# RWKV-7 chunk steps: the state kept in U's half of the tile, brought into the bank of its update by identity products

## The chip, the cores and the metric

One core of a Trainium2 chip runs the whole kernel. The metric is the device time of one execution in microseconds; the median of three runs is given. The engines are TensorE (matmuls and transposes, results in PSUM), VectorE, ScalarE, GpSimd and the DMA queues. PSUM has 8 banks of 128 partitions by 512 fp32 values here, shared by all stages through one pool.

## The reference

A trunk of two layers over 512 tokens of width 1024: an RG-LRU block, a conv-MLP, an RWKV-7 time-mixing block, a second conv-MLP, a final norm. The change lies in the RWKV-7 scan, 16 heads of 64:

```python
def step(S, inp):
    r_t, w_t, k_t, v_t, a_t, b_t = inp
    sa = jnp.einsum('bhij,bhj->bhi', S, a_t)
    S = S * w_t[:, :, None, :] + sa[..., None] * b_t[:, :, None, :] + v_t[..., :, None] * k_t[..., None, :]
    y = jnp.einsum('bhij,bhj->bhi', S, r_t)
    return S, y
```

## The kernel before

**The scan in chunks.** The 512 tokens are cut into 8 chunks of 64. Within a chunk the recurrence is written with matrices: a triangular system per head and chunk, solved beforehand (`solve`, whose inverse stands in `LTs`), gives U, the rows that the old state contributes through `a`; then y and the new state are products with U, v and the old state. The heads are handled in halves H (8 heads each) and each half in two groups g of 4 heads. Group 1 runs one step behind group 0, so there are 17 steps n = 0 to 16, and step n handles chunk n of group 0 and chunk n - 1 of group 1 (8 chunks of H = 0, then 8 of H = 1). Chunks of even and odd number use opposite halves of the 128 partitions (`q`), so that a state written in one step is read in place in the next.

**One step.** `step(n)` issues, in this order:
- `pe` (L1206): 8 products, 128 rows by 64 columns, of the masked matrix `W` with the tile `sv`, which has v in one half of its partitions and the state S in the other. ScalarE copies the result to `e1` (L1209).
- `prep_begin` and `prep_s` for step n + 1: 64-row products `s` (L1160) into two banks, which VectorE multiplies with masks into the next `W` (L1167).
- `fill(0)`: work of other stages that is spread over the steps. Three lanes of generators hold it: the v projection of the second half and the first half of the output projection (`acc`), the solve of H = 1, which has long rows of small VectorE operations (L1041, L1043), the bonus terms (`bon`) and the gate (`pgt`). `fills` says how many pieces of each lane go into each of a step's three places.
- `pu` (L1222) and the first products of `py` (L1225), 64 rows by 64 columns, alternating; `py` reads the state from `sv`. ScalarE copies `pu` into `tu` as U (L1229).
- `prep_t` for step n + 1: four transposes `tr` (L1174), ScalarE's copies of them to `tok` (L1176), of `rts` (L1180), of v beside U (L1183), and VectorE's copy of v into the next `sv` (L1184).
- `fill(1)`.
- `pd` (L1238): the update of the state by U and v, 8 products. VectorE adds the old state (L1247) and multiplies with the decay (L1248) into the next `sv`; after a first chunk, where the state is zero, it multiplies straight out of PSUM (L1250).
- The last products of `py` (L1254), and ScalarE's copies of `py` to `ytok` (L1258).
- `between()`, which advances the tail of earlier chunks (group norm, `mu`, `var`, `ytok`, `pz`), and `fill(2)`.

**The order.** The Tile framework turns this program into one static list for each engine. Operations keep roughly the program's order; one that is ready earlier can be placed ahead of others, except where `keep_in_program_order` ties it. Every engine runs its list in order, and semaphores follow from what tiles are read and written. PSUM tiles of the pool share 8 banks, so a new tile waits for a bank to come free.

The tiles that matter: `svs`, two state-and-v tiles; `W` and `tu` for each step, from a pool of 21 buffers, `tu` holding `tok` and `uv` (v in one half of the partitions, U in the other).

Of the kernel before, what the change touches and what calls it, by code (L numbers as in the profile page):

```python
# [7 lines left out]
F32 = mybir.dt.float32  # L8
F32R = mybir.dt.float32r
AF = mybir.ActivationFunctionType  # L10
ALU = mybir.AluOpType
# [4 lines left out]
P = 128  # L16
# [5 lines left out]
C = 64  # L22
NC = T // C
# [18 lines left out]
class Kernel:  # L42
# [1042 lines left out]
    def rwkv_chunks(self, pool, mv, AR, BK, PC, selk, LTs, again):  # L1085
# [9 lines left out]
        nc, tc, I = self.nc, self.tc, self.I  # L1095
        V = self.x.rearrange("p k t -> p (k t)").rearrange("p (c n) -> p c n", c=4)
        half = lambda i: slice(i * 64, i * 64 + 64)

        svs = [pool.tile([P, 4, 2, C], F32, name=f"sv{i}") for i in range(2)]
        rts = pool.tile([P, 4, C], F32, name="rts")  # L1100
        e1 = pool.tile([P, 2, 2, C], F32, name="e1")
        decay = pool.tile([P, KB, 2, NC], F32, name="decay")
# [15 lines left out]
        sets, ytok = {}, {}  # L1118
# [11 lines left out]
        def groups(n):  # L1130

            out = []
            for g in range(2):
                m = n - g
                if 0 <= m < 2 * NC:
                    H, c = m // NC, m % NC
                    out.append((g, slice(2 * g, 2 * g + 2), H, c, c // 2, c % 2))
            return out

        def prep_begin(n):  # L1140
            W, tu = self.b4(F32, (2, 4, P), "W"), self.b4(F32, (2, 4, P), "tu")
            sets[n] = (W, tu[:, 0], tu[:, 1])
            for g, bs, H, c, c2, q in groups(n):
                if c == 0:
                    nc.gpsimd.memset(svs[n % 2][half(1 - q), bs], 0.0)

        def prep_s(n):
            gs = groups(n)
            W = sets[n][0]
            pss = [four(self.bank("s")) for _ in range(2)]  # L1150

            for i in range(2):
                for part in range(3):
                    for g, bs, H, c, c2, q in gs:
                        for h in range(2):
                            b, z = 2 * g + i, 1 - q if part else q
                            row = slice(q * P + z * C, q * P + z * C + C)
                            col = (slice(0, P), half(q), half(1 - q))[part]
                            w = self.ident[half(h), half(h)] if part == 2 else BK[H][half(h), b, c2, row]
                            nc.tensor.matmul(pss[h][half(z), b, col], w, AR[H][half(h), b, c2, q * P + col.start : q * P + col.stop],  # L1160
                                             start=True, stop=True, tile_position=(h * 64, z * 64))

            q0, g0, k = gs[0][5], gs[0][0], len(gs)
            mask = masks[:, q0 : q0 + k].rearrange("p q z t -> p q (z t)").unsqueeze(2).to_broadcast([P, k, 2, P])
            two = lambda t: t[:, 2 * g0 : 2 * (g0 + k)].rearrange("p (g i) t -> p g i t", i=2)
            for h in range(2):
                nc.vector.tensor_tensor(two(W[:, h]), two(pss[h]), mask, ALU.mult)  # L1167
        def prep_t(n):
            gs = groups(n)
            W, tok, uv = sets[n]  # L1170
            pt = four(self.bank("tr"))
            for g, bs, H, c, c2, q in gs:
                for i in range(2 * g, 2 * g + 2):
                    nc.tensor.transpose(pt[:, i, :], BK[H][:, i, c2, q * P : (q + 1) * P], self.ident)  # L1174
            bs = slice(gs[0][1].start, gs[-1][1].stop)
            nc.scalar.copy(tok[:, bs], pt[:, bs])  # L1176
            for g, bs, H, c, c2, q in gs:
                bh = half(1 - q)

                nc.scalar.copy(rts[bh, bs], AR[H][half(q), bs, c2, q * P + q * C : q * P + (q + 1) * C])  # L1180
                n0 = H * 512 + g * 256
                v = V[half(q), c2, n0 : n0 + 256].rearrange("p (i t) -> p i t", t=P)
                nc.scalar.copy(uv[half(q), bs], v)  # L1183
                nc.vector.tensor_copy(svs[n % 2][half(q), bs].rearrange("p i h t -> p i (h t)"), v)  # L1184

        def fill(i):
            for lane in range(3):
                self.background(self.fills[lane][i], lane)

        def step(n, between):  # L1190
            gs = groups(n)
            W, tok, uv = sets.pop(n)
            sv = svs[n % 2]
            more = n < 2 * NC

            heads = [(i, h, G) for i in range(2) for h in range(2) for G in gs]

            late = [(i, h, G) for i in range(2) for h in range(2) for G in gs[::-1]]
            chained = lambda first, ins: ins if first else tc.keep_in_program_order(ins)
            by_head = lambda ps: ps[:, 0:256].rearrange("p (i h t) -> p i h t", h=2, t=C)  # L1200
            flat = lambda t: t.rearrange("p i h t -> p i (h t)")

            pe = by_head(self.bank("pe"))
            for n_, (i, h, (g, bs, H, c, c2, q)) in enumerate(late):
                bh = half(1 - q)
                chained(n_ == 0, nc.tensor.matmul(pe[bh, i, h], W[:, h, 2 * g + i, bh], sv[:, 2 * g + i, h], start=True, stop=True,  # L1206
                                                  tile_position=(0, 64 - q * 64)))
            of = slice(0, P) if len(gs) == 2 else half(1 - gs[0][5])
            nc.scalar.copy(e1[of], pe[of])  # L1209

            if more:
                prep_begin(n + 1)
                prep_s(n + 1)
            if n == NC + 1:

                between()
            fill(0)

            pu, py = by_head(self.bank("pu")), by_head(self.bank("py"))
            for i, h, (g, bs, H, c, c2, q) in heads:  # L1220
                kh, bh, b = half(q), half(1 - q), 2 * g + i
                nc.tensor.matmul(pu[bh, i, h], LTs[H][bh, c2 * 8 + b * 2 + h, :], e1[bh, i, h], start=True, stop=True,  # L1222
                                 tile_position=(64 - q * 64, 64 - q * 64))
                r = rts[bh, b] if h == q else AR[H][bh, b, c2, q * P + q * C : q * P + q * C + C]
                tc.keep_in_program_order(nc.tensor.matmul(py[kh, i, h], r, sv[bh, b, h], start=i + h == 0, stop=False,  # L1225
                                                          tile_position=(64 - q * 64, q * 64)))
            for g, bs, H, c, c2, q in gs:
                bh = half(1 - q)
                nc.scalar.copy(uv[bh, bs], flat(pu[bh]))  # L1229
            if more:  # L1230
                prep_t(n + 1)
            fill(1)
            if any(c < NC - 1 for g, bs, H, c, c2, q in gs):
                pd = by_head(self.bank("pd"))
                live = [x for x in late if x[2][3] < NC - 1]
                for n_, (i, h, (g, bs, H, c, c2, q)) in enumerate(live):
                    b = 2 * g + i
                    chained(n_ == 0, nc.tensor.matmul(pd[half(1 - q), i, h], tok[:, b, half(h)], uv[:, b, half(h)], start=True, stop=True,  # L1238
                                                      tile_position=(0, 64 - q * 64)))
                for g, bs, H, c, c2, q in gs:  # L1240
                    if c == NC - 1:
                        continue
                    kh, bh = half(q), half(1 - q)
                    Sn = svs[1 - n % 2][kh, bs]
                    w = decay[:, H * 4 + 2 * g : H * 4 + 2 * g + 2, :, c : c + 1].to_broadcast([P, 2, 2, C])
                    if c:
                        nc.vector.tensor_tensor(Sn, pd[bh], sv[bh, bs], ALU.add)  # L1247
                        nc.vector.tensor_tensor(Sn, Sn, w[kh], ALU.mult)  # L1248
                    else:
                        nc.vector.tensor_tensor(Sn, pd[bh], w[bh], ALU.mult)  # L1250
            for n_, (i, h, (g, bs, H, c, c2, q)) in enumerate(late):
                kh, b = half(q), 2 * g + i
                chained(n_ == 0 and not any(c < NC - 1 for _, _, _, c, _, _ in gs),
                        nc.tensor.matmul(py[kh, i, h], W[:, h, b, kh], uv[:, b, half(h)], start=False, stop=i + h == 2, tile_position=(0, q * 64)))  # L1254
            for g, bs, H, c, c2, q in gs:
                if g == 0 and q == 0:
                    ytok[H, c2] = pool.tile([P, 4, P], F32, tag="ytok", name="ytok", bufs=3)
                nc.scalar.copy(ytok[H, c2][half(q), bs], flat(py[half(q)]))  # L1258
            between()
            fill(2)  # L1260
# [265 lines left out]
```

## Time and profile before

| what | value |
|---|---|
| median of 3 runs | 1327.06 us (1325.48 to 1329.35) |
| profiled execution, its own time | 1328.46 us |
| its span | 1326.7 us |
| TensorE (PE) busy | 1295.2 us, 98% |
| VectorE (DVE) busy | 860.3 us, 65% |
| ScalarE (ACT) busy | 614.0 us, 46% |
| mean granted clock of TensorE | 0.992 |

Busy times of TensorE come from records of which two belong to one fp32 matmul; records overlap, so starts tell more than durations. Times inside the trace count from the span's start. A figure in brackets behind a row is the idle time of that engine before it, with the instruction that ended it.

### The profile page before, as it was taken

Reading aid. Unit: us, or ns where it says so; the run is one execution under the profiler, and the core shown is the slowest. Engines: PE = TensorE matmul, PEld = TensorE weight load, DVE = VectorE, ACT = ScalarE, POOL = GpSimd, SP = SyncE. Lnnn points to the kernel's source line nnn. Section 1 sums busy time; section 2 is a strip of 40 time slices with the busy share of each in tenths; the row PEclk is TensorE's granted clock in tenths of the full one; section 3 lists DMA queues with packets and bytes.
Section 4 is the critical chain, followed back from the end, with each engine's and each line's share of the span. In section 5 each row is a group of like instructions: output and inputs, shape, how many; then the busy total and the mean of one; then the engine's idle time right before and its main releaser. Section 6 shows DMA issues by size and latency. Waiting matters only on the chain.

```text
span 1326.7 us, 20245 instructions
## 1 busy us (share of the span) xinstructions
PE 1295.2 (98%) x8339; PEld 1055.3 (80%) x8339; DVE 860.3 (65%) x1332; ACT 614.0 (46%) x968; POOL 67.9 (5%) x110
## 2 busy tenths in 40 slices
PE   8999999999999999999999988799999999999998
PEld 7877888888888888876678877678888888888886
DVE  5998656455436655497989787877565555365523
ACT  6797444333224423368843668555533332244311
POOL 4000000000000000020010011120000000000000
PEclk8999999999999999999999999899999999999999
DMA  5423333323333433213212112133323223333311
GB/s 183 126 64 96 96 111 96 95 64 96 95 96 95 127 115 120 88 32 116 86 48 72 58 38 80 42 89 91 99 89 109 67 95 95 96 96 127 112 64 64
DMA packets 72124, 120.27 MB, mean 91 GB/s; under 512 B 9498, under 2 KB 21476, under 8 KB 71904
## 3 DMA queue, kind: packets, MB, share of 16 engines
q1 hardware_dynamic: 70672, 117.20, 28.7%
q8 instruction: 65, 1.06, 0.3%
q10 hardware_dynamic: 576, 1.05, 0.2%
q0 software_dynamic: 784, 0.74, 0.2%
q14 instruction: 27, 0.22, 0.1%
HBM read 114.44 MB, written 4.52 MB: 90 GB/s over the span
## 4 chain that ended last, share of the span: by engine, by line
PE 88%; DVE 6%; ACT 3%; issue 1%; DMA 1%; POOL 0%; SPq 0%; POOLq 0%; DVEq 0%; ACTq 0%
PE acc L51 22%; PE acc L53 22%; PE acc L52 22%; PE acc L616 3%; PE acc L615 3%; PE acc L617 3%; PE s L1160 1%; PE acc L989 1%; PE acc L990 1%; PE acc L991 1%; PE pe L1206 1%; DVE W L1167 1%; DMA xin<-in_x_dram 1%; DVE X L1043 1%; DVE sv L1248 1%
## 5 line engine op out<-in xcount | busy, mean ns | idle before, releaser
L51 PE MATMUL acc<-xs,wh 128*128 128x512 f32 x896 | 352.0, 393 | 0.0
L53 PE MATMUL acc<-xs,wl 128*128 128x512 f32 x896 | 348.9, 390 | 0.7 <-DVE wl L91 0.7
L52 PE MATMUL acc<-xs,wh 128*128 128x512 f32 x896 | 349.6, 390 | 0.0
L91 DVE TENSOR_TENSOR wl<-raw,wh 128x1024 fp32r<-128x1024 f32 (+1 forms) x201 | 242.9, 1216 | 163.4 <-PE acc L52 95.0
L90 ACT CAST wh<-raw 128x1024 fp32r<-128x1024 f32 (+1 forms) x201 | 207.9, 1045 | 257.7 <-DVE wl L91 169.6
L53 PEld LDWEIGHTS acc<-xs,wl 128*128 128x128 f32 x896 | 168.5, 188 | 36.8 <-DVE wl L91 1.2
L51 PEld LDWEIGHTS acc<-xs,wh 128*128 128x128 f32 x896 | 168.8, 188 | 35.0 <-ACT wh L90 0.2
L52 PEld LDWEIGHTS acc<-xs,wh 128*128 128x128 f32 x896 | 168.7, 188 | 34.5 <-DVE wl L91 0.2
L576 DVE SCALAR_TENSOR_TENSOR cv<-gpad,pv,cv 128x512 f32<-128x512 f32 x96 | 71.9, 749 | 22.2 <-ACT cv L574 21.1
L90 ACT CAST hid<-un 128x512 fp32r<-128x512 f32 x48 | 29.8, 620 | 108.7 <-DVE un L583 108.7
L616 PE MATMUL acc<-wh,hid 128*128 128x512 f32 (+1 forms) x200 | 76.8, 384 | 0.0
L615 PE MATMUL acc<-wh,hid 128*128 128x512 f32 (+1 forms) x200 | 76.5, 382 | 0.0
L617 PE MATMUL acc<-wl,hid 128*128 128x512 f32 (+1 forms) x200 | 75.9, 380 | 0.0
L52 PE MATMUL acc<-hid,wh 128*128 128x512 f32 x192 | 75.7, 394 | 0.0
L53 PE MATMUL acc<-hid,wl 128*128 128x512 f32 x192 | 75.6, 394 | 0.0
L51 PE MATMUL acc<-hid,wh 128*128 128x512 f32 x192 | 75.5, 393 | 0.0
L582 DVE TENSOR_TENSOR un<-acc,rb 128x512 f32<-128x512 f32 x48 | 33.1, 689 | 44.3 <-PE acc L53 44.3
L91 DVE TENSOR_TENSOR hid<-un,hid 128x512 fp32r<-128x512 f32 x48 | 33.2, 691 | 31.5 <-ACT hid L90 31.5
L574 ACT ACTIVATE cv<-gpad,pv 128x512 f32<-128x512 f32 x48 | 39.2, 817 | 20.3 <-DVE gpad L571 20.1
L578 ACT ACTIVATE ge<-cv 128x512 f32<-128x512 f32 x48 | 30.1, 627 | 35.6 <-DVE cv L576 35.6
L620 DVE TENSOR_TENSOR xtok<-xtok,acc 128x512 f32<-128x512 f32 (+1 forms) x25 | 16.7, 666 | 44.9 <-PE acc L617 44.9
L615 PEld LDWEIGHTS acc<-wh,hid 128*128 128x128 f32 x200 | 37.5, 188 | 8.0
(425 smaller groups left out, 2176.1 us busy)
## 6 DMA issues: line engine op xcount, KB each, us to landing
raw<-in_ffn_w_up_dram SPq DMA_DIRECT2D x96, 512.0 KB, 3.9
raw<-in_ffn_w_down_dram SPq DMA_DIRECT2D x48, 512.0 KB, 3.7
raw<-in_rwkv_w_rkv_dram SPq DMA_DIRECT2D x24, 512.0 KB, 3.8
raw<-in_lru_w_in_dram SPq DMA_DIRECT2D x16, 512.0 KB, 3.9
raw<-in_lru_w_out_dram SPq DMA_DIRECT2D x8, 512.0 KB, 3.8
raw<-in_rwkv_w_out_dram SPq DMA_DIRECT2D x8, 512.0 KB, 3.4
xd<-x SPq DMA_DIRECT2D x8, 256.0 KB, 2.0
AR<-xd SPq DMA_DIRECT2D x1, 2048.0 KB, 9.1
```

Of the source, the lines that this page charges most:

```text
L51: nc.tensor.matmul(ps, wh, xh, start=start, stop=False)
L52: nc.tensor.matmul(ps, wh, xl, start=False, stop=False)
L53: nc.tensor.matmul(ps, wl, xh, start=False, stop=stop)
L90: (self.nc.vector.tensor_copy if dve else self.nc.scalar.copy)(hi, src)
L91: self.nc.vector.tensor_tensor(lo, src, hi.bitcast(F32), ALU.subtract)
L574: nc.scalar.activation(cv, gp[:, 0:T], AF.Identity, bias=self.vec(f"ffn_conv_b{l}", fb), scale=cw(0))
L576: nc.vector.scalar_tensor_tensor(cv, gp[:, j : j + T], cw(j), cv, ALU.mult, ALU.add)
L578: nc.scalar.activation(ges[o], cv, AF.Gelu_apprx_tanh)
L582: nc.vector.tensor_tensor(un, ps, rbs[0], ALU.mult)
L615: nc.tensor.matmul(ps, hh[:, s], wh[:, k, m], start=kk == 0, stop=False)
L616: nc.tensor.matmul(ps, hl[:, s], wh[:, k, m], start=False, stop=False)
L617: nc.tensor.matmul(ps, hh[:, s], wl[:, k, m], start=False, stop=kk == 7)
```

## The change

The separate tiles `svs` go. The state S now stands in `uv`, in the half of the partitions where U of the same step will be written; `pe` and the first products of `py` read it there, beside v, which ScalarE already copies into `uv`. VectorE's copy of v goes. Before `pu`, 64-row products with the identity put S into the bank `pd` (for groups that have a state and another chunk to come); the later products of U and v accumulate onto it, so the addition L1247 goes, and one VectorE product with the decay writes the new state from PSUM into the next step's `uv`. The memset that clears the state at a first chunk writes to the next `tu`.

```diff
-        svs = [pool.tile([P, 4, 2, C], F32, name=f"sv{i}") for i in range(2)]
...
         def prep_begin(n):
-            W, tu = self.b4(F32, (2, 4, P), "W"), self.b4(F32, (2, 4, P), "tu")
-            sets[n] = (W, tu[:, 0], tu[:, 1])
+            W, tu = self.b4(F32, (2, 4, P), "W"), self.b4(F32, (2, 4 * P), "tu")
+            sets[n] = (W, *(tu[:, i].rearrange("p (i t) -> p i t", t=P) for i in range(2)))
             for g, bs, H, c, c2, q in groups(n):
                 if c == 0:
-                    nc.gpsimd.memset(svs[n % 2][half(1 - q), bs], 0.0)
+                    nc.gpsimd.memset(tu[half(1 - q), 1, bs.start * P : bs.stop * P], 0.0)
...
                 nc.scalar.copy(uv[half(q), bs], v)
-                nc.vector.tensor_copy(svs[n % 2][half(q), bs].rearrange("p i h t -> p i (h t)"), v)
...
-                chained(n_ == 0, nc.tensor.matmul(pe[bh, i, h], W[:, h, 2 * g + i, bh], sv[:, 2 * g + i, h], start=True, stop=True,
+                chained(n_ == 0, nc.tensor.matmul(pe[bh, i, h], W[:, h, 2 * g + i, bh], uv[:, 2 * g + i, half(h)], start=True, stop=True,
...
             fill(0)
+
+            live = [x for x in late if x[2][3] < NC - 1]
+            if live:
+                pd = by_head(self.bank("pd"))
+            for i, h, (g, bs, H, c, c2, q) in live:
+                kh, bh = half(q), half(1 - q)
+                if c:
+                    nc.tensor.matmul(pd[kh, i, h], self.ident[bh, bh], uv[bh, 2 * g + i, half(h)], start=i + h == 0, stop=False,
+                                     tile_position=(64 - q * 64, q * 64))
...
-                tc.keep_in_program_order(nc.tensor.matmul(py[kh, i, h], r, sv[bh, b, h], start=i + h == 0, stop=False,
+                tc.keep_in_program_order(nc.tensor.matmul(py[kh, i, h], r, uv[bh, b, half(h)], start=i + h == 0, stop=False,
...
             fill(1)
-            if any(c < NC - 1 for g, bs, H, c, c2, q in gs):
-                pd = by_head(self.bank("pd"))
-                live = [x for x in late if x[2][3] < NC - 1]
-                for n_, (i, h, (g, bs, H, c, c2, q)) in enumerate(live):
-                    b = 2 * g + i
-                    chained(n_ == 0, nc.tensor.matmul(pd[half(1 - q), i, h], tok[:, b, half(h)], uv[:, b, half(h)], start=True, stop=True,
-                                                      tile_position=(0, 64 - q * 64)))
-                for g, bs, H, c, c2, q in gs:
-                    if c == NC - 1:
-                        continue
-                    kh, bh = half(q), half(1 - q)
-                    Sn = svs[1 - n % 2][kh, bs]
+            for n_, (i, h, (g, bs, H, c, c2, q)) in enumerate(live):
+                b = 2 * g + i
+                chained(n_ == 0, nc.tensor.matmul(pd[half(q), i, h], tok[:, b, half(h)], uv[:, b, half(h)], start=c + i + h == 0, stop=i + h == 2,
+                                                  tile_position=(0, q * 64)))
+            for g, bs, H, c, c2, q in gs:
+                if c < NC - 1:
+                    kh = half(q)
                     w = decay[:, H * 4 + 2 * g : H * 4 + 2 * g + 2, :, c : c + 1].to_broadcast([P, 2, 2, C])
-                    if c:
-                        nc.vector.tensor_tensor(Sn, pd[bh], sv[bh, bs], ALU.add)
-                        nc.vector.tensor_tensor(Sn, Sn, w[kh], ALU.mult)
-                    else:
-                        nc.vector.tensor_tensor(Sn, pd[bh], w[bh], ALU.mult)
+                    Sn = sets[n + 1][2][kh, bs].rearrange("p i (h t) -> p i h t", h=2)
+                    nc.vector.tensor_tensor(Sn, pd[kh], w[kh], ALU.mult)
```

## Rows read from the trace of the kernel before

**Rows 1.** The page's slices: busy tenths in 40 equal parts of the span.

```profile
PE   8999999999999999999999988799999999999998
DVE  5998656455436655497989787877565555365523
```

**Rows 2.** Windows from `pe` to `pe`, steps 1 and 14: busy us of each engine.

```profile
core 0: us, PE busy (x) PEld busy (x) DVE busy (x) ACT busy (x) POOL busy (x), PEclk, DMA share, GB/s
...
747.07:757.34 10.27, 8.60 (x160) 6.19 (x159) 9.67 (x24) 5.25 (x12) 0.00 (x0) 1.00 0.21 73
...
866.97:874.57 7.60, 7.60 (x148) 5.94 (x149) 6.86 (x13) 5.16 (x13) 0.00 (x0) 1.00 0.46 140
```

**Rows 3.** Waits, 738 to 887 us: us in total, times, longest.

```profile
ACT rts L1180 <- PE py L1225: 13.3, 11, 2.9
...
PE pe L1206 <- DVE sv L1248: 6.7, 7, 2.9
```

**Rows 4.** Timeline of TensorE: start, us, line, out<-in, count, idle time before.

```profile
757.34 0.87 PE L1206 MATMUL pe<-sv,W 128*64 128x64 f32 x12 [1.67 <-DVE sv L1250]
...
779.06 1.08 PE L1206 MATMUL pe<-sv,W 128*64 128x64 f32 x16 [2.95 <-DVE sv L1248]
...
799.39 0.69 PE L1206 MATMUL pe<-sv,W 128*64 128x64 f32 x16 [0.69 <-DVE sv L1248]
...
803.70 1.20 PE L1065 MATMUL m1p<-XN,O 32*32 32x32 f32 x64 [1.51 <-DVE XN L1048]
...
831.68 1.12 PE L1288 MATMUL pz<-ident,ytok 128*128 128x128 f32 x4 [2.94 <-DVE ytok L1283]
...
851.25 0.69 PE L1206 MATMUL pe<-sv,W 128*64 128x64 f32 x16 [1.88 <-DVE sv L1248]
```

**Rows 5.** Groups of instructions, 738 to 887 us: count, busy us, mean ns, idle before.

```profile
L1248 DVE TENSOR_TENSOR sv<-sv,decay 64x256 f32<-64x256 f32 x24 | 10.6, 440 | 0.6
...
L1247 DVE TENSOR_TENSOR sv<-pd,sv 64x256 f32<-64x256 f32 x24 | 10.1, 422 | 9.3 <-PE pd L1238 8.8
...
L1184 DVE COPY sv<-x 64x256 f32<-64x256 f32 x28 | 9.3, 331 | 3.3 <-PE pe L1206 2.8
...
L1250 DVE TENSOR_TENSOR sv<-pd,decay 64x256 f32<-64x256 f32 x4 | 1.7, 426 | 0.6 <-PE pd L1238 0.5
```

**Rows 6.** Timeline of VectorE, end of step 1.

```profile
756.32 0.42 DVE L1247 TENSOR_TENSOR sv<-pd,sv 64x256 f32<-64x256 f32 x1
756.77 0.43 DVE L1250 TENSOR_TENSOR sv<-pd,decay 64x256 f32<-64x256 f32 x1
```

**Rows 7.** Timeline of TensorE, steps 0 and 2.

```profile
740.06 0.68 PE L1206 MATMUL pe<-sv,W 128*64 128x64 f32 x8
...
740.67 0.56 PE L1160 MATMUL s<-AR,BK 64*64 64x128 f32 x16
...
762.21 0.27 PE L1222 MATMUL pu<-e,LT 64*64 64x64 f32 x1
...
762.83 0.66 PE L1174 MATMUL tr<-ident,BK 128*128 128x128 f32 x4
...
764.13 0.69 PE L1238 MATMUL pd<-tu 128*64 128x64 f32 x16
...
764.64 0.64 PE L1254 MATMUL py<-tu,W 128*64 128x64 f32 x16
```

**Rows 8.** Timeline of ScalarE, step 4.

```profile
782.73 0.30 ACT L1180 COPY rts<-AR 64x128 f32<-64x128 f32 x1 [1.12 <-PE py L1225]
783.04 0.74 ACT L1229 COPY tu<-pu 64x256 f32<-64x256 f32 x2
...
787.44 0.82 ACT L1183 COPY tu<-x 64x256 f32<-64x256 f32 x2
```

**Rows 9.** Windows after two of the gaps; the third figure from the end is the granted clock.

```profile
757.30:762.20 4.90, 4.80 (x74) 4.34 (x74) 4.71 (x10) 1.36 (x4) 0.85 (x1) 0.65 0.35 110
...
779.00:784.00 5.00, 4.74 (x106) 4.38 (x108) 2.31 (x5) 2.63 (x6) 1.99 (x2) 0.66 0.01 3
```

**Rows 10.** Timelines of TensorE and VectorE in step 4: the transposes, the mask products.

```profile
782.74 0.66 PE L1174 MATMUL tr<-ident,BK 128*128 128x128 f32 x4
...
786.62 1.28 DVE L1167 TENSOR_TENSOR W<-s,masks 128x512 f32<-128x512 f32 x2
```

More of the change, by code (lines that the diff above doesn't have):

```diff
@@ L1192, in step @@
             W, tok, uv = sets.pop(n)
-            sv = svs[n % 2]
             more = n < 2 * NC
@@ L1232, in step @@
             fill(1)
-            if any(c < NC - 1 for g, bs, H, c, c2, q in gs):
-                pd = by_head(self.bank("pd"))
-                live = [x for x in late if x[2][3] < NC - 1]
-                for n_, (i, h, (g, bs, H, c, c2, q)) in enumerate(live):
-                    b = 2 * g + i
-                    chained(n_ == 0, nc.tensor.matmul(pd[half(1 - q), i, h], tok[:, b, half(h)], uv[:, b, half(h)], start=True, stop=True,
-                                                      tile_position=(0, 64 - q * 64)))
-                for g, bs, H, c, c2, q in gs:
-                    if c == NC - 1:
-                        continue
-                    kh, bh = half(q), half(1 - q)
-                    Sn = svs[1 - n % 2][kh, bs]
-                    w = decay[:, H * 4 + 2 * g : H * 4 + 2 * g + 2, :, c : c + 1].to_broadcast([P, 2, 2, C])
-                    if c:
-                        nc.vector.tensor_tensor(Sn, pd[bh], sv[bh, bs], ALU.add)
-                        nc.vector.tensor_tensor(Sn, Sn, w[kh], ALU.mult)
-                    else:
-                        nc.vector.tensor_tensor(Sn, pd[bh], w[bh], ALU.mult)
+            for n_, (i, h, (g, bs, H, c, c2, q)) in enumerate(live):
[5 more added lines that the diff above has]
+                    kh = half(q)
+                    w = decay[:, H * 4 + 2 * g : H * 4 + 2 * g + 2, :, c : c + 1].to_broadcast([P, 2, 2, C])
+                    Sn = sets[n + 1][2][kh, bs].rearrange("p i (h t) -> p i h t", h=2)
+                    nc.vector.tensor_tensor(Sn, pd[kh], w[kh], ALU.mult)
             for n_, (i, h, (g, bs, H, c, c2, q)) in enumerate(late):
                 kh, b = half(q), 2 * g + i
-                chained(n_ == 0 and not any(c < NC - 1 for _, _, _, c, _, _ in gs),
+                chained(n_ == 0 and not live,
                         nc.tensor.matmul(py[kh, i, h], W[:, h, b, kh], uv[:, b, half(h)], start=False, stop=i + h == 2, tile_position=(0, q * 64)))
```

## The prediction

> **What bounds the kernel now.** I read the page's slices first [rows 1]: TensorE is at nine tenths nearly everywhere, but falls to 8, 8 and 7 in the slices from 763 to 862 us, where VectorE stands at 7 and 8. That is where the RWKV steps are: 17 steps, from the first `pe` products at 740.06 us to the last at 881.20 us. No engine is full throughout, so the stage has to be read step by step.
>
> Windows cut at the `pe` products give that; two of the sixteen are shown [rows 2]. In step 1 VectorE is busy for 9.67 of 10.27 us and TensorE for 8.60; up to step 3 and in steps 5, 6, 11 and 12 VectorE is busy for 94 to 98%. In step 14 TensorE is full, and after the steps it stays so to the end: what the stage saves, the end saves.
>
> The list of waits names what TensorE waits for [rows 3]: the state product L1248, seven times, 6.7 us. The timeline places it [rows 4]: `pe` begins after idle gaps of 1.67 us (step 2, behind L1250, the same product for a first chunk), 2.95 (step 4), 0.69 (step 6) and 1.88 (step 12). Four smaller gaps make up the rest of the 6.7, 1.2 us. Two more gaps end in VectorE: 1.51 us before the solve's `m1p` in step 6 and 2.94 before `pz` in step 9.
>
> **What is removed.** In the stage, 24 additions (L1247) of 422 ns and 28 copies of v (L1184) of 331 ns mean [rows 5]: 10.1 + 9.3 = 19.4 us of VectorE. With its spacing an addition takes 0.45 us (starts at 756.32 and 756.77 [rows 6]), and a copy, most of which take 0.28 us, about 0.30. A step with two additions loses 1.5 us of VectorE, step 1, with one, 1.05. All of them stand ahead of the next state product in VectorE's queue. Where VectorE is full the step can shorten by all of this; where it is not, only the additions count, which lie between `pd` and `pe`.
>
> **What is added.** Identity products, 4 for each group that has a state: 24 times, 96 products, in 14 steps (1 to 7 and 9 to 15). The nearest rows are `pd` and the `py` behind it, 8 products each in two parts of the array, two records a product: `pd` begins at 764.13, `py` at 764.64 [rows 7], so 0.51 us for 16 records. One group alone is no cheaper: its `pe`, 8 records, takes from 740.06 to 740.67, 0.61 us. From below, `pu` and the early `py`, 32 records in four parts, take 0.62 us (762.21 to 762.83), which is 0.31 for 16. I take 0.51, since the identity products use only the two parts that early `py` uses. For 14 steps: 4.3 us from below, 7.1 taken, 8.5 from above, and nothing where TensorE idles anyway.
>
> The state product now reads `pd` in PSUM. The kernel has four of that kind already, L1250: 426 ns mean, against 440 for L1248 [rows 5]. I take no difference. [...]
>
> **What is moved or newly waited for.** The state stands in U's half, so the U copy (L1229) must also wait for `pe`, the early `py` and the identity products. On ScalarE the copy to `rts` waits for that `py` already, 11 times [rows 3], and in step 4, at 782.73, it stands right ahead of U [rows 8]. So the new wait ends with a product that ScalarE waits for anyway. Behind U in ScalarE's queue are the `tok` copy and the next `rts`; they come no later for it than `pu` itself does. I take zero. The copy of v beside U (L1183) now precedes `pe` of the next step: the tightest case is two copies that start at 787.44 and last 0.82 [rows 8], ending 0.57 us before `pe` at 788.83. With that cover gone `pe` would wait for ScalarE. The memset that clears the state goes to a fresh tile on GpSimd; no instruction waits for it before. No DMA is issued or moved. The bank of `pd` is held from before `pu`: nothing here, weighed below.
>
> **The sum, by step.** A step's new length is the longer of TensorE's time plus 0.51 and VectorE's less 1.5.
> - Where TensorE waited for VectorE: step 1, min(1.05, 1.67 - 0.51) = 1.05. Step 3, min(1.50, 2.95 - 0.51) = 1.50. Steps 5 and 6 together, 0.69 + 1.51 less two identity groups = 1.2 (VectorE's 3.0 suffices). Step 11, min(1.5, 1.88 - 0.51) = 1.37. Together 5.1 us.
> - Where TensorE had little idle time, steps 2, 4, 7, 10 and 12 to 15: 8 x 0.51, less the small gaps of 1.2 us and one of 0.15 before step 5 that the profile gives to the sequencer: 2.7 us lost.
> - Step 9: `pd` waits there for a ScalarE that is busy, which covers the identity products, and two copies go from ahead of the reductions whose result `pz` waits for: 0.5 us gained.
> - The clock. [...] By the terms above the first gap shrinks to 0.11 us, the second to 0.94. I count the first loss as gone and the second as halved: 2.5 us gained. Bounds 0 and 3.4.
>
> 5.1 - 2.7 + 0.5 + 2.5 = 5.4 us. The profiled execution took 1328.46 us (its span is 1326.7), so 1323.1; it lies 1.4 us above the runs' median of 1327.06, hence 1321.7, rounded to **1322 us**.
>
> **The rivals.**
> *TensorE takes it back.* The identity products cost 0.61 each time, 1.4 us more in 14 steps, and the clock falls as before: 5.1 - 2.7 + 0.5 - 1.4 = 1.5 us gained, 1325.6. For it: `pe`, which other shapes follow, takes 0.61 where `pd`, which its own shape follows, takes 0.51 [rows 7]. Against it: as written the identity products have the shape of `pu` behind them. [...]
>
> *VectorE held up more.* All the idle time that ended in the state products and in `m1p` closes (6.7 + 1.67 + 1.51 = 9.9), half of that before `pz` (1.5) and both clock losses (3.4), less 7.1 for the identity products: 7.7 us, and more if other orders on VectorE follow: 1317 to 1319. Against it: in steps 3 and 11 the removed work is smaller than the gap.
>
> *A ninth PSUM bank: slower.* With `pd`'s bank held from before `pu`, those held when `tr` asks for its own are two of `s`, two of `acc`, `pu`, `py` and `pd`: seven, and `tr` takes the eighth and last. If one more is held there (`bon`, as in step 1), TensorE stops at `tr` until VectorE's mask product frees a bank of `s`. That comes late: in step 4 `tr` starts at 782.74, the two mask products at 786.62 for 1.28 us [rows 10]. To the middle of the two, less the additions of 0.9 us, this is 3.6 us; three more steps of that kind (1, 5 and 6) make some 3.4. The gains of steps 3, 5 and 6 go, and half of the clock's stays (1.3): 1.05 + 1.37 + 0.5 + 1.3 - 2.7 - 7.0 = 5.5 us lost, 1332.5. It decides as soon as a ninth bank is wanted in steps 4 to 6. Against it: the count gives eight, and `tr` never has a gap before it now. [...]
>
> **How the numbers follow.** Forecast 0.43 (own range 1319 to 1325), TensorE takes it back 0.25, VectorE held up more 0.17, the ninth bank 0.15. A measurement of this kernel tells about 0.3%, 4.0 us, from no change: faster is below 1323.1, slower above 1331.0. Faster: two thirds of the forecast (0.29), the second rival, a little of the first (0.04): 0.50. Slower: most of the bank's share, 0.13. The rest, 0.37, is the same. The range reaches into both outer rivals, 1316 to 1331; it also holds the bounds of the identity products (2.8 us less, 1.4 more) and of the clock (0.9 less, 2.5 more).
>
> **What would show it.** Right: no L1247 and L1184 in VectorE's groups; identity products of about 0.5 us a step ahead of `pu`; the gaps before `pe` in steps 2, 4, 6 and 12 shorter by 1 to 2 us; a clock of 1.00 after step 2; steps 14 and 15 longer by half a microsecond. Wrong: `tr` behind the mask product; `pe` waiting for ScalarE's copy of v; the clock lost in other steps; or an order on VectorE that puts other work where the additions stood, so that the state product comes no earlier.

## The result, and the profile after

The changed kernel takes 1332.26 us (median of 6 runs, 1331.91 to 1334.16), the kernel before 1327.59 in the runs beside it: ratio 1.0038 [1.0025, 1.0051], the 95% interval in brackets. It is slower by 4.7 us, a little more than the 0.3% that a measurement tells. The forecast was 1322 (1316 to 1331): wrong in sign, and the time lies outside the range. The profiled execution took 1333.34 us, its span is 1331.6.

The page of the changed kernel, its slices (answering to [rows 1]), with TensorE's granted clock in the third line:

```profile
PE   8999999999999999999999989899999999999998
DVE  5988756565436655497997874768565555365523
PEclk9999999999999999999999997999999999999999
```

VectorE is relieved, TensorE is not emptier, and one slice has a clock of 7 tenths (the lowest of the kernel before has 8). Windows of the changed kernel, first the whole stage from the first `pe` to the last, then steps 1, 3, 5, 6 and 14 (columns as in [rows 2]):

```profile
738.67:886.01 147.34, 133.54 (x2763) 112.83 (x2762) 101.56 (x190) 91.00 (x218) 22.73 (x19) 0.93 0.17 56
...
745.85:755.93 10.08, 9.23 (x168) 6.76 (x167) 9.54 (x23) 5.25 (x12) 0.00 (x0) 1.00 0.23 72
764.78:778.02 13.24, 10.16 (x180) 9.38 (x180) 9.25 (x21) 8.07 (x15) 4.58 (x4) 0.87 0.18 53
786.41:792.87 6.46, 5.91 (x161) 5.33 (x160) 6.14 (x12) 4.12 (x10) 1.64 (x1) 1.00 0.01 3
792.87:815.58 22.71, 20.00 (x323) 18.44 (x323) 12.05 (x16) 13.50 (x29) 2.21 (x3) 0.70 0.08 26
871.08:879.06 7.98, 7.98 (x166) 6.37 (x165) 5.58 (x9) 5.11 (x13) 0.00 (x0) 1.00 0.44 136
```

The same stage of the kernel before, with its steps 6, 3 and 5:

```profile
740.06:881.20 141.14, 123.04 (x2572) 102.14 (x2571) 119.00 (x240) 91.42 (x219) 22.57 (x19) 0.95 0.19 59
...
799.39:809.41 10.02, 8.48 (x276) 7.57 (x276) 9.55 (x15) 7.01 (x18) 0.31 (x1) 1.00 0.02 4
767.15:779.06 11.91, 8.96 (x171) 8.25 (x171) 11.35 (x29) 7.04 (x14) 2.65 (x2) 1.00 0.31 89
788.83:799.39 10.56, 8.57 (x169) 7.99 (x170) 10.27 (x19) 8.91 (x17) 1.63 (x1) 1.00 0.17 53
```

Such rows can be cut into three parts: idle time of TensorE (length less PE busy), time lost to the clock (length times one less the granted clock, taken step by step), and what is left, its work at full clock. The forecast's own parts are 7.1 us of work for the identity products and 2.5 gained from the clock; for its sum of 5.4 gained, idle time had to fall by 10.0.

| us from `pe` to `pe`, steps 0 to 15 | length | idle | clock | work | rest of the span |
|---|---|---|---|---|---|
| before | 141.1 | 18.1 | 6.8 | 116.3 | 1185.6 |
| after | 147.3 | 13.8 | 10.2 | 123.3 | 1184.3 |
| difference | +6.2 | -4.3 | +3.4 | +7.0 | -1.3 |
| forecast | -5.4 | -10.0 | -2.5 | +7.1 | 0 |

The work grew about as forecast. The idle time fell by less than half of what was needed, and the clock got worse. The split is rough, to some 2 or 3 us in its parts: low clock during idle time counts twice, and small products take less than twice as long at half the clock (64 records of `m1p` last 1.20 and 1.47 us in step 6 before, 1.92 in the slow stretch after). The lengths are firm. By stretches, step 3 is longer by 1.3 us, steps 5 and 6 together by 8.6; steps 1 and 2 are shorter by 1.1, step 4 by 1.4, steps 9 to 12 by 2.8, and the others make +1.6. So the loss has two places, and in steps 5 and 6 it is the clock: their idle time together is 3.5 us before and 3.3 after, their clock loss 0 and 6.8.

**Step 3.** The timelines of the changed kernel, first ScalarE, then VectorE, then TensorE:

```profile
770.68 1.04 ACT L1052 COPY LT<-LT 32x1024 f32<-32x1024 f32 x1 [3.31 <-DVE LT L1046]
771.75 0.30 ACT L1179 COPY rts<-AR 64x128 f32<-64x128 f32 x1
772.07 0.76 ACT L1235 COPY tu<-pu 64x256 f32<-64x256 f32 x2
```

```profile
768.71 1.94 DVE L1046 STREAM_TRANSPOSE LT<-X 128x1024 f32<-128x1024 f32 x1
774.28 1.29 DVE L1166 TENSOR_TENSOR W<-s,masks 128x512 f32<-128x512 f32 x2 [3.63 <-PE py L1252]
775.61 0.88 DVE L1248 TENSOR_TENSOR tu<-pd,decay 64x256 f32<-64x256 f32 x2
```

```profile
768.29 0.22 PE L1231 MATMUL py<-tu,rts 64*64 64x64 f32 x1
...
772.88 0.69 PE L1241 MATMUL pd<-tu 128*64 128x64 f32 x16 [3.08 <-ACT tu L1235]
```

VectorE's freed time goes to the solve: its transpose into LT (L1046) starts at 768.71, against 773.96 before. ScalarE's copy of that result now stands ahead of `rts` and U in ScalarE's list. U's products and the early `py` are done by 768.5, but ScalarE stands idle for 3.31 us for the solve, then copies LT for 1.04, and only then U. TensorE waits 3.08 us, and VectorE, out of other work, waits 3.63. Before, U came first:

```profile
770.69 0.75 ACT L1229 COPY tu<-pu 64x256 f32<-64x256 f32 x2
776.65 1.04 ACT L1052 COPY LT<-LT 32x1024 f32<-32x1024 f32 x1
```

**Step 6.** TensorE in the changed kernel:

```profile
798.79 0.34 PE L1241 MATMUL pd<-tu 128*64 128x64 f32 x4 [0.51 <-ACT tu L1235]
801.16 1.88 PE L1065 MATMUL m1p<-XN,O 32*32 32x32 f32 x32 [2.04 <-DVE XN L1048]
802.97 0.48 PE L1241 MATMUL pd<-tu 128*64 128x64 f32 x4
803.39 1.91 PE L1065 MATMUL m1p<-XN,O 32*32 32x32 f32 x32
805.23 0.69 PE L1241 MATMUL pd<-tu 128*64 128x64 f32 x8
```

The solve's `m1p` stands inside `pd`, so a quarter of `pd` is done and the rest waits behind `m1p`, which waits for VectorE's transpose (799.02, 2.00 us). That is not new in kind: in the kernel before, `m1p` stood ahead of all of `pd` and waited for the same transpose, 1.51 us at 803.70 [rows 4]:

```profile
804.83 0.69 PE L1238 MATMUL pd<-tu 128*64 128x64 f32 x16
```

But before, the clock stayed at 1.00 in this step, and now it falls. Windows of one microsecond, and of the stretch between:

```profile
800.00:801.00 1.00, 0.00 (x0) 0.00 (x0) 1.00 (x2) 0.60 (x2) 0.00 (x0) 0.98 0.00 0
801.00:802.00 1.00, 0.83 (x16) 0.87 (x17) 1.00 (x3) 0.00 (x0) 0.00 (x0) 0.50 0.00 0
...
814.00:815.00 1.00, 1.00 (x8) 1.00 (x7) 0.00 (x0) 0.00 (x0) 1.00 (x2) 0.69 0.00 0
...
801.00:814.00 13.00, 12.84 (x180) 12.22 (x181) 4.24 (x9) 6.10 (x14) 0.63 (x2) 0.50 0.01 3
```

For 13 us TensorE is busy at a granted clock of 0.50; the step loses 6.8 us (0.30 of 22.71). The list also moved work between the steps: of the projection's products (`acc`), step 5 has 37 before and 12 after, step 6 has 11 before and 42 after.

The waits after (answering to [rows 3]), in three lines:

```profile
DVE tu L1248 <- PE pd L1241: 15.1, 8, 3.8
...
PE pd L1241 <- ACT tu L1235: 4.9, 5, 3.1
...
PE pe L1203 <- DVE tu L1248: 2.7, 4, 0.9
```

The same wait of `pd` in the kernel before:

```profile
PE pd L1238 <- ACT tu L1229: 4.9, 6, 1.5
```

The wait for the state product fell from 8.4 us (6.7, and 1.67 that ended in L1250 [rows 4]) to 2.7. `pd`, one product earlier in the same chain, waits 4.9 us for ScalarE in both kernels, but not in the same places: after, 3.08 of it is the gap of step 3, so in the other steps the wait fell to 1.8.

### The profile page after: what moved, and what is told of

Its sections match the earlier page's. It is cut to its first block, busy times and chain, and to the rows that moved or that the text cites. A ratio compares the mean times of both kernels' runs of the same rounds, so it can differ in the third digit from the quotient of the medians.

```text
span 1331.6 us, 20583 instructions
## 1 busy us (share of the span) xinstructions
PE 1305.3 (98%) x8531; PEld 1065.4 (80%) x8531; DVE 841.0 (63%) x1276; ACT 613.8 (46%) x968; POOL 68.3 (5%) x110
## 3 DMA queue, kind: packets, MB, share of 16 engines
q10 hardware_dynamic: 576, 1.05, 0.2%
## 4 chain that ended last, share of the span: by engine, by line
PE 89%; DVE 6%; ACT 3%; issue 1%; DMA 1%; POOL 0%; SPq 0%; POOLq 0%; ACTq 0%; DVEq 0%
PE acc L51 22%; PE acc L53 22%; PE acc L52 22%; PE acc L616 3%; PE acc L615 3%; PE acc L617 3%; PE acc L989 1%; PE acc L991 1%; PE acc L990 1%; PE s L1159 1%; DVE DA L1041 1%; DVE X L1043 1%; DVE W L1166 1%; PE m1p L1065 1%; DMA xin<-in_x_dram 1%
```

## The experiments

The theory after the result: the two parts are worth about what was forecast, and the rest is lost to the order of the static lists (theory A). Its rivals: the identity products cost more than their 0.5 us a step, or the bank held early costs something, or relief of VectorE is worth nothing.

**The products alone.** The kernel before, with the identity products added into unused columns of `py`'s bank; nothing reads them.

```diff
+            for i, h, (g, bs, H, c, c2, q) in late:
+                kh, bh = half(q), half(1 - q)
+                if 0 < c < NC - 1:
+                    nc.tensor.matmul(px[kh, i, h], self.ident[bh, bh], sv[bh, 2 * g + i, h], start=i + h == 0, stop=i + h == 2,
+                                     tile_position=(64 - q * 64, q * 64))
```

> The kernel before, with the 96 identity products added ahead of pu into the unused columns of py's bank, where nothing reads them; additions and copies of v stay. It prices the identity products without an early bank and without relief of VectorE. Theory A (TensorE pays 0.5 us in each of 14 steps, and the rest of the loss is static order and clock): TensorE's work in the steps, idle time and clock taken out, grows by 7 us, and the time by 4 to 8 us over before, a little less where TensorE had idle time. Theory B (the early bank of pd is what hurts): the products fill idle time, the time grows by 0 to 3 us.

Measured: 1334.34 us, 1.0039 [1.0022, 1.0056], 6.1 us more than before. Work in the stage 122.4 us, 6.1 more than before.

**The bank held early.** The same products, in the bank of `pd`, which is taken ahead of `pu`.

```diff
+            if live:
+                pdb = self.bank("pd")
+                px = pdb[:, 256:512].rearrange("p (i h t) -> p i h t", h=2, t=C)
...
-                pd = by_head(self.bank("pd"))
+                pd = by_head(pdb)
```

> The same as the run with the products in py's bank, except that they go into the unused columns of pd's bank, which is therefore held from ahead of pu as in the changed kernel. Theory A: within 2 us of that run. Theory B: 4 us or more above it, with tr or m1p waiting for a bank.

Measured: 1336.44 us, 1.0056 [1.0041, 1.0072]: 2.1 us above the run before it, at the edge of theory A's 2 us. The two stages differ by 2.3 us, of which 1.8 is clock loss in step 6 (3.5 against 1.7). TensorE stops once at `tr` until a mask product of VectorE, 0.74 us in step 1, as the rival of the ninth bank has it; `pe` of step 2 then waits 0.48 us, where it waits 1.28 with the products in `py`'s bank. So an early bank costs some 2 us here, and no more.

**The relief alone.** The kernel before without the additions and without VectorE's copies of v.

```diff
...
-                nc.vector.tensor_copy(svs[n % 2][half(q), bs].rearrange("p i h t -> p i (h t)"), v)
...
-                        nc.vector.tensor_tensor(Sn, pd[bh], sv[bh, bs], ALU.add)
-                        nc.vector.tensor_tensor(Sn, Sn, w[kh], ALU.mult)
+                        nc.vector.tensor_tensor(Sn, pd[bh], w[bh], ALU.mult)
```

> The kernel before without the 24 additions and without VectorE's copies of v, and without identity products: the old state and v are left out of the recurrence, so only its time counts. It prices VectorE's relief alone, 19 us of VectorE in the steps. Theory A: 3 to 10 us faster than before, since idle time of TensorE closes; less if the clock falls in step 6 as in the changed kernel. Theory C (VectorE's work was hidden, the identity products explain all): within 2 us of before.

Measured: 1323.25 us, 0.9955 [0.994, 0.9971], 5.0 us less. Work in its stage comes out at 119.3 us, though it has the products of the kernel before, 116.3: so far off can the split be.

**The change without its products.**

```diff
                 if c:
-                    nc.tensor.matmul(pd[kh, i, h], self.ident[bh, bh], uv[bh, 2 * g + i, half(h)], start=i + h == 0, stop=False,
-                                     tile_position=(64 - q * 64, q * 64))
+                    pass
...
```

> The changed kernel without its 96 identity products, which leaves the old state out of the update; pd's bank is still taken ahead of pu. Theory A: TensorE's work in the steps falls by 7 us; the time by 4 to 8 us against the changed kernel, to 1324 to 1328, if the low clock of step 6 stays. Theory B: the early bank stays, so the low clock and most of the loss stay: 1329 or more. Theory C: as fast as before or a little faster, 1326 to 1328, with no low clock in step 6.

Measured: 1325.29 us, 0.9972 [0.9956, 0.9988], 7.0 less than the changed kernel; work in the stage 116.4 us. Yet it is 2.0 us slower than the relief alone, at the edge of what the runs can tell, and its step 6 still loses 5.1 us to the clock, where the profiled execution of the relief alone loses nothing there. From these four: the products cost 6 to 7 us, the relief gives 5.0, and 6.1 - 5.0 = 1.1 is not 4.7, though each of these figures has an interval of 1 or 2 us to either side. Most of the rest is not in the parts. Next, the two places.

**The solve's first product later.** In the changed kernel the generator of the solve lets two turns of its lane pass ahead of `m1p`.

```diff
+        for _ in range(2 * H):
+            yield 1
```

> The changed kernel with the solve's m1p products issued two turns of their lane later, so that in step 6 pd, the late py, pz and six acc products stand ahead of them while VectorE makes XN; nothing else differs up to there. Theory A (idle time of TensorE ahead of m1p lets the clock fall for 13 us, which costs 6.8 us): the gap of 2.0 us ahead of m1p closes, the granted clock in step 6 stays at 0.95 or more, and the time is 1324 to 1328. Theory D (the identity products and the moved acc work are what step 6 pays for): 1330 to 1333, whatever the clock does.

Measured: 1326.14 us, 0.9981 [0.9969, 0.9992], 6.1 less than the changed kernel. Step 6 takes 13.08 us in place of 22.71, with a clock of 1.00; step 3 is as slow as it was (13.28).

**ScalarE's LT copies later.** In the changed kernel they are tied behind U of step 6.

```diff
+        for _ in range(H):
+            yield 1
...
-            nc.scalar.copy(LT[hi, :, 32:64], LT[hi, :, 0:32])
+            put = self.tc.keep_in_program_order if H else lambda ins: ins
+            put(nc.scalar.copy(LT[hi, :, 32:64], LT[hi, :, 0:32]))
```

> The changed kernel with the solve's two LT copies on ScalarE tied behind the U copy of step 6 in program order, so that none stands ahead of U in step 3. Theory A (a copy that waits for VectorE's transposition holds U up by 3 us in step 3, and the clock falls behind it): the gap of 3.08 us ahead of pd in step 3 falls below 0.5, the clock loss behind it goes, step 3 takes 9 to 10 us, and the time falls by 2 to 5 us to 1327 to 1330; step 6 keeps its low clock. Theory E (something else than ScalarE's order makes pd wait): step 3 stays at 13 us.

Measured: 1324.72 us, 0.9974 [0.996, 0.9988], 7.5 less than the changed kernel. Step 3 takes 8.62 us in place of 13.24 and TensorE is never idle in it; step 6 (18.96) still loses 3.4 us to the clock. That is more than the 2 to 5 us expected: the turn that passes ahead of the copies puts `m1p` one turn later too, and 3.8 us of the gain are in step 6, 4.6 in step 3.

**More filling work in the middle steps**, with `m1p` later, in the changed kernel and in the kernel before: the rates of the projection's pieces go up.

```diff
...
-        self.fills = ((1.2, 1.1, 0.2), (1.0, 0.9, 1.9), (1.3, 1.8, 2.0))
+        self.fills = ((1.2, 1.1, 0.2), (1.0, 1.6, 1.9), (1.3, 2.4, 2.0))
```

> The changed kernel with the rates of the v projection raised (0.9 and 1.8 pieces to 1.6 and 2.4 in the second and third place of a step), so that 24 of its products no longer stand behind the solve's in step 6, and with m1p two turns later. Theory A: no stretch of low clock in step 6, 1322 to 1327. Theory D: 1330 to 1333, since all the work is still there.

> The kernel before with the same rates and the same later m1p: what this order is worth without the change. If the order of before was already good, as theory A says: 1325 to 1330. If it gains as much as the changed kernel does by it, the order has nothing to do with the change: 1322 or less.

Measured: 1329.66 us, 1.0003 [0.9991, 1.0015], and 1330.35, 1.0011 [0.9996, 1.0026]. The gain expected of the first did not come. In both, about 5 us go to the clock in step 6 (5.18 and 5.12), behind 3.0 and 4.0 us of idle time in step 5. More filling work early does not help here.

**Both edits of order** (the LT copies one turn later and tied, `m1p` two turns later in all), in the changed kernel and, as a control, in the kernel before.

> The changed kernel with both edits of order: ScalarE's copies of the solve's transposed triangle behind the copy of U of step 6, and the solve's first product two lane turns later. Theory A (the loss is the two stalls of the order, in steps 3 and 6, and the clock that falls behind them; the change itself is worth about +1 us): the two gains add in part, steps 3 and 6 come to about 8.6 and 10 to 13 us, little clock loss, 1319 to 1323 us. Theory B (the stalls move: one edit's gain comes back as another stall): no faster than the better of the single edits, 1324 to 1327 us.

> The kernel before with the same two edits, a control. Theory A (the order of before had neither stall): no gain, 1326 to 1330 us. Theory B (later copies and a later product help whatever the change): faster here too, by as much as in the changed kernel, 1320 to 1324 us.

Measured: 1320.91 us (4 runs, 1320.37 to 1321.62), 0.9946 [0.9929, 0.9962], and 1329.21, 1.0012 [0.9998, 1.0026]. Theory A's numbers hold in both: the changed kernel gains 11.4 us and is faster than either kernel, the kernel before gains nothing. Its reason for the second does not hold in full: the order of before did have `m1p` ahead of `pd` in step 6, and what it lacked was the clock loss. The edits do move things there too: step 6 takes 8.03 us in place of 10.02, step 7 11.32 in place of 9.04. Windows of the changed kernel with both edits, the stage and its steps 3 and 6:

```profile
738.84:874.29 135.45, 126.64 (x2764) 105.77 (x2763) 101.78 (x190) 90.73 (x218) 22.68 (x19) 0.97 0.19 61
...
764.98:773.60 8.62, 8.62 (x181) 7.95 (x181) 8.13 (x19) 4.74 (x12) 2.66 (x2) 1.00 0.17 49
788.44:801.55 13.11, 12.11 (x258) 10.90 (x258) 11.27 (x14) 12.60 (x26) 2.20 (x3) 1.00 0.14 42
```

**Relief without products.** The kernel before with the second copy of v on GpSimd, without and with the edits of order.

```diff
-                nc.vector.tensor_copy(svs[n % 2][half(q), bs].rearrange("p i h t -> p i (h t)"), v)
+                nc.gpsimd.tensor_copy(svs[n % 2][half(q), bs].rearrange("p i h t -> p i (h t)"), v)
```

> The kernel before with VectorE's second copy of v made by GpSimd instead; the additions stay and there are no identity products. VectorE is relieved of the copies alone and TensorE pays nothing. Theory A (relief of VectorE without the products is worth up to the 5 us that the run without additions and copies gained): 1324 to 1327 us. Theory B (the order moves against it, or GpSimd's copy is late and holds up the update): 1328 to 1333 us.

> The kernel before with the copy of v on GpSimd and both edits of order. Theory A: the edits of order take away what stalls the freed VectorE makes, 1320 to 1325 us. Theory B (no stall to take away): within 1 us of the run with the copy on GpSimd alone.

Measured: 1330.09 us, 1.0015 [1.0004, 1.0025], and 1329.88, 1.0021 [1.001, 1.0031]. Theory A's gain came in neither; both came out as theory B said. VectorE is busy for 114.92 us in the stage, only 4.1 less than before, though 9.3 us of copies are gone (see the last section), and the edits add nothing. The additions, which lie between `pd` and `pe`, are all still there, so the run does not price the relief of the change.

## Why the prediction was wrong

**What held.** The identity products, roughly: 7.1 us forecast within 4.3 to 8.5, 7.0 as work (123.3 - 116.3, a rough split), 6.1 as time when they were added alone. Steps 14 and 15, where the clock is 1.00 and TensorE has no idle time, have grown by 0.38 and 0.32 us, for 0.51 forecast, which would be 5 us in 14 steps. The state product from PSUM, U's new wait and the early bank were put at nothing. The groups and the order of the changed kernel bear the first out:

```profile
L1248 DVE TENSOR_TENSOR tu<-pd,decay 64x256 f32<-64x256 f32 x28 | 11.8, 420 | 15.5 <-PE pd L1241 15.1
...
L1222 PE MATMUL pd<-tu,ident 64*64 64x64 f32 x192 | 9.4, 223 | 0.0
```

The product takes 420 ns from PSUM, against 440 from SBUF [rows 5]: no extra cost shows. ScalarE's copy of U waited for the early `py` once, 1.4 us in step 14, where TensorE has no idle time. `tr` has no gap before it in steps 4 to 6, so the ninth bank is not why the kernel got slower, though a loss was what that rival forecast; the one gap before a `tr`, 1.52 us in step 9, stands where `pd` waited 1.55 us before. "TensorE takes it back" failed in its price: the products are not dearer than taken.

**The step that failed** is the rule of the sum, "A step's new length is the longer of TensorE's time plus 0.51 and VectorE's less 1.5". It takes the freed time out of each step and leaves every list in its old order. The lists are made anew for the changed program, and they took the time for the solve; with it failed the clock's term, which had a gain of 0 to 3.4 us and no room for a loss:

- Step 1: forecast 1.05 shorter, measured 0.19. VectorE is still busy for 9.54 of 10.08 us, and `pe` of step 2 still waits 0.85 us for the state product.
- Step 3: forecast 1.50 shorter, measured 1.33 longer. The gap of 2.95 before `pe` [rows 4] is gone, and one of 3.08 before `pd` has come.
- Steps 5 and 6: forecast 1.2 shorter, measured 8.6 longer: 6.8 by the clock, the rest by work, of which the identity products are 1.
- Step 11: forecast 1.37 shorter, measured 0.52.
- The clock: its term starts from 1.7 us lost behind each of the gaps of 1.67 and 2.95 us [rows 4], where the clock is short by 0.35 over 4.90 us and by 0.34 over 5.00 [rows 9]. The loss behind the gap of step 1 is gone, as forecast; that behind step 3 stayed (1.72 us, now within the step), and 6.8 us came in step 6. Behind the gap before `pz`, in steps 9 and 10, 1.7 us were gained (3.4 lost before, 1.7 after), which the sum had left out. In all 3.4 us were lost, where 2.5 were to be gained.
- Left out of the sum as well: `pd`'s own waits for ScalarE, 4.9 us before, which it counts in step 9 alone. It puts step 10, with 1.48 us of idle time, 1.10 of it before `pd`, among the steps with little. With the clock, steps 9 and 10 came out 2.3 us shorter together, for 0.4 forecast; that gain is luck.

The prediction named, among what would make it wrong, "an order on VectorE that puts other work where the additions stood, so that the state product comes no earlier". That came about in step 1, but the list had no price for it, and the dear part of step 3 was one step further: what VectorE finished earlier also moved its follower on ScalarE ahead of the recurrence.

**That the order decides is shown** by the single edits and the pair with both. Without them the change makes the kernel 4.7 us slower, with both 8.3 faster (1329.21 to 1320.91). In step 3 the mechanism is shown too: with the copies tied behind U, the gap before `pd` and the clock loss behind it are gone. In step 6 it is shown that a later `m1p` takes the loss away, and that the loss is clock; it is not shown that the place of `m1p` is what the change made worse, since it stood ahead of `pd` before as well.

With both edits the stage comes out near the sum: work +7.0, idle -9.3, clock -3.4, together -5.7 (135.4 - 141.1), for -5.4 forecast. Step by step it does not: step 3 is 3.3 us shorter, for 1.5 forecast, steps 1 and 11 are 0.2 and 0.5 shorter, for 1.05 and 1.37, and `pd`'s wait for ScalarE is down to 1.8 us. So the agreement in total is partly luck.

**Open** is by what rule the framework placed the LT copy and `m1p` where it did, and why TensorE's clock fell to 0.50 in step 6 and stayed there for 13 us, when in the kernel before it was 1.00 throughout the step. It wasn't shown either what makes the changed kernel without its products slower than the relief alone, beyond the clock of its step 6.

## What to carry to other kernels

Where lists are made from the program by a scheduler, the time that an engine is relieved of can go to whatever else can run on it, and the followers of that work may then stand ahead of the critical chain on other engines. A sum over the old order is a forecast for that order alone. When a change that should pay doesn't, look in each in-order list for an instruction of a side lane just ahead of one of the chain, tie it behind, and time that beside the same edit in the kernel before. Give the clock a term with both signs: here a step with 2.7 us of idle time lost 6.8 us more to it.

## What the runs showed of the hardware

**The clock.** In the changed kernel it falls to 0.50 at 801 us, after gaps of 0.51 and 2.04 us with four records of `pd` between, and stays there for over 13 us in which TensorE is busy for 12.84 of 13.00 us: first `m1p` and `pd`, products of 32 and 64 columns, then `pz` and `acc`; it rises in the window from 814 to 815 (0.69), with `acc` products running. In the kernel before, step 6 has gaps as well, the longest 1.51 us [rows 4], and its clock is 1.00 throughout. The idle time alone does not tell the loss: in seven of the profiled runs step 6 has 2.6 to 3.1 us of it, and the clock loss there is 6.8 us in the changed kernel, 5.1 without its products, 3.4 with the LT copies later, 3.5 and 1.7 in the two runs with the products alone, 1.7 with the copy on GpSimd, and none in the relief alone:

```profile
791.98:807.42 15.44, 12.76 (x307) 11.62 (x306) 12.17 (x15) 12.32 (x26) 0.31 (x1) 1.00 0.12 37
```

Each of these is one execution, and executions of one kernel differ: of 83 of the kernel before, the 30 with a mean granted clock of 0.994 or more took 1325.2 to 1328.5 us, the 13 with 0.989 took 1330.8 to 1331.8. The one of the relief alone has 0.998, the other seven 0.992 to 0.995, so its step 6 may not be typical. After the gap of 3.08 us in step 3 the loss is 1.72 us, as after the gaps of before [rows 9].

**GpSimd beside VectorE.** The copies of v, 331 ns each on VectorE [rows 5], take 553 on GpSimd, and some of VectorE's instructions grow longer. Groups of the kernel with the copy on GpSimd, and timelines of its GpSimd and VectorE:

```profile
L1184 POOL COPY sv<-x 64x256 f32<-64x256 f32 x28 | 15.5, 553 | 83.8 <-PE pe L1206 83.1
...
L1283 DVE TENSOR_TENSOR ytok<-ytok,bv 128x512 f32<-128x512 f32 x6 | 5.1, 855 | 0.2
```

```profile
757.66 1.18 POOL L1184 COPY sv<-x 64x256 f32<-64x256 f32 x2 [9.77 <-PE pe L1206]
...
757.98 0.61 DVE L1043 TENSOR_TENSOR X<-X,DA 128x247 f32<-128x247 f32 x1
...
768.62 1.04 POOL L1275 TENSOR_TENSOR bv<-x,bon 128x512 f32<-128x512 f32 x1
...
768.74 1.07 DVE L1041 TENSOR_TENSOR DA<-DA,X 128x135 f32<-128x135 f32 x1
```

The same kinds of VectorE instruction in the kernel before:

```profile
L1283 DVE TENSOR_TENSOR ytok<-ytok,bv 128x512 f32<-128x512 f32 x6 | 4.1, 686 | 0.1
```

```profile
759.87 0.42 DVE L1043 TENSOR_TENSOR X<-X,DA 128x247 f32<-128x247 f32 x1
...
771.14 0.30 DVE L1041 TENSOR_TENSOR DA<-DA,X 128x135 f32<-128x135 f32 x1
```

With 28 copies gone VectorE is busy for 4.1 us less, not 9.3; added up by instruction, those that are left take some 4 us more, and the remainder is overlap, which busy time counts once. Not all of it is beside the copies: the longest stretch in these rows lies beside GpSimd's product L1275, which the new order has put there. The product on VectorE begins 0.12 us after GpSimd's, takes 1.07 us in place of 0.30, and ends 0.15 us after it. In the first pair the product, which begins inside two copies, grew by 0.19 us and ends 0.25 us before them. Why they grow longer isn't shown by these rows.
